# Indices of the first four heads made ahead, and the first gathers moved to the end of the wq stage

## The chip, the cores and the metric

The kernel runs on one core of a Trainium2 chip. The metric is the device time of one execution in microseconds (us); lower is better. The core has five engines, each with an instruction stream of its own that it works through in order: TensorE (PE) multiplies matrices, VectorE (DVE) and ScalarE (ACT) work element by element, GpSimd (POOL) here issues gathers, and SyncE (SP) issues plain loads. Sixteen DMA engines move the data. PEld in a profile is the loading of weights into PE.

## The reference

One layer of a diffusion backbone. Its last part, the one that matters here, is a retrieval network over 256 tokens `ht` with 8 heads and the 16 best experts of 16384 for each head and token:

```python
q = (ht @ wq).reshape(n, PEER_HEADS, 2, PEER_DK // 2)
s = jnp.einsum('nhpc,pkc->nhpk', q, keys)
s1, i1 = lax.top_k(s[:, :, 0], 16)
s2, i2 = lax.top_k(s[:, :, 1], 16)
cand = (s1[..., :, None] + s2[..., None, :]).reshape(n, 8, 256)
sc, ci = lax.top_k(cand, 16)
e = take(i1, ci // 16) * 128 + take(i2, ci % 16)      # 128 experts per token
gate = softmax(sc)
a = jnp.einsum('nd,nhkd->nhk', xb, u_tab[e])          # dots with rows of u
w = gate * gelu(a)
out = jnp.einsum('nhk,nhkd->nd', w, v_tab[e])         # weighted rows of v
```

Tables u and v have 16384 rows of 2048 floats (8 KB a row).

## The kernel before

All arithmetic is in float32; a matrix product is made from a high part (`hi`, an ACT copy to a shorter format) and a low part (`lo`, a DVE subtraction) of each weight block. The stages follow each other: modulation, mixers, output projection `wout`, and then

- **wq**: 16 strips of `wq` (two halves each). After each strip its scores against the keys are made, and DVE takes the best 16 (`score_top`, `pair_top`). When strip 8 is done, `gen_look(1, 0, ...)` turns the best pairs of the first four heads of token block 1 into expert numbers (`e12`).
- **the dense stage**: for 192 of the 256 tokens (`NA`) the dots with all rows of u are made on PE, in 128 rounds that are called rows below. A row needs 1 MB of `u_t`, which comes as two halves; each half takes an ACT instruction that makes `hi` and a DVE instruction that makes `lo` (three `hi` and three `lo` buffers). PE does 16 matmuls with `hi` and 16 with `lo` for a row (tile `ups`); ACT (`ut`) and DVE (`W<-ut,ups`) then store the result in row i2 of the large tile W.
- beside it, the **gathered tokens**: the other 64 tokens, the last of block 1, go in two groups of 32 through 32 steps each. A step u gathers 128 rows of u (1 MB, `DMA_INDIRECT` on POOL) and takes their dot with `hB` on DVE (a SCALAR_TENSOR_TENSOR of 128x2048, called a dot below); a step v gathers 128 rows of v and multiplies them on PE into `adaps` or `yb`. Eight steps u come first, then steps u and v alternate. `gen_route(1, ...)` makes the expert numbers of the last four heads, the list of indices `idx` and the gates, and then starts `gen_gather`.
- **the tail**: for each of the 192 tokens one gather of 128 rows of v and four matmuls (`y`).

What stands where is set when the program is written, by a clock of estimated PE time: generators ("lanes") give up control with a number of microseconds, and their next instructions are put behind the PE work that stands at that time (`spawn`, `pump`, `advance`). Each engine then has a fixed list.

W is filled row by row, so its still empty parts ("rooms" of 2048 columns, 10.67 rows each) hold other things: `wides` is the list of places for a row of u_t, and `gaths` that for gathers. Before the change, rooms 0, 4, 6, 8, 9 (`LENT_1`) and a place of its own (`g1`) hold u_t rows 0 to 5 first, which are loaded beside wq, one per strip (`ahead`), and rooms 1, 2, 3, 5, 7 (`LENT_U`) rows 6 to 10. When its first row is used up, a `LENT_1` place or `g1` becomes a place for gathers.

`gen_gather` spreads its steps evenly up to the estimated end of the dense stage, `R["u_end"]`, which `open_w` sets when the dense stage begins. A gather is issued when its place is free; SP holds the loads in the order of the list.

Of the kernel before, what the change touches and what calls it, by code (L numbers as in the profile page):

```python
# [23 lines left out]
F32 = mybir.dt.float32  # L24
F32R = mybir.dt.float32r
BF16 = mybir.dt.bfloat16
I32 = mybir.dt.int32
U32 = mybir.dt.uint32
AF = mybir.ActivationFunctionType
OP = mybir.AluOpType  # L30
PSUM = bass.MemoryType.PSUM

P = 128
D = 2048
KD = D // P
T = 256
# [4 lines left out]
NK = 128  # L41
PH = 8
TOPK = 16
NB = 64
NA = T - NB
BT = 32
REP = P // BT
STEPS = PH * TOPK // REP
# [15 lines left out]
HY3 = 6.0  # L64
HY4 = 3.0
LOOK_AT = 8
LOOK_Y = 3.0
ITY = 6.0
BIGB = 3
VWY = 7.0  # L70
# [66 lines left out]
class Slots:  # L137
# [11 lines left out]

        self.slots.append([pool, tag, F32, None, True, free, None])  # L150

    def place(self, owner, view, last=None, free=None):

        self.slots.append([owner, view, None, None, True, free, last])

    def over(self, owner):

        return all(s[3] is not None and self.done(s[3]) for s in self.slots if s[0] == owner)

    def take(self, unit):  # L160
        for s in self.slots:
# [21 lines left out]
def build(tc, a, stack, dbg=None):  # L183
# [6 lines left out]
    def open_pool(name, side="left", **kw):  # L190
        cm = tc.tile_pool(name=name, bufs=1, side=side, reuse_waits="tile", **kw)
        return cm, cm.__enter__()
# [120 lines left out]
    def spawn(lane, gen, front=False):  # L313
        q = lanes.setdefault(lane, collections.deque())
        (q.appendleft if front else q.append)([clock["t"], gen])
# [721 lines left out]
    R = {}  # L1037
    gaths = Slots(lambda u: u.used, 2048)


    LENT_1 = (0, 4, 6, 8, 9)
    LENT_U = (1, 2, 3, 5, 7)
    LENT = (4, 6, 8, 9, 10, 11)
    x1d = tc.dram_tile([P, KD, T], F32, name="x1_spill")
# [1 line left out]
    def make_hf(u):  # L1046
        drain(only=("ada",))
        x1 = Y["x"]
        ss = mm_ps("ss1")
        mm(ss[:, 0:T], ones, Y["sq"], start=True, stop=False)  # L1050
        mm(ss[:, 0:T], ones, Y["last"], start=False, stop=True)
        prepare()
        rs = con.tile([P, T], F32, name="rs1", tag="rs1")
        rstd_of(rs, ss[:, 0:T], D)
        araws.drop(V["B"])
        close_pool(V["pb"])
        R["rh"] = open_pool("rh", side="right")
        R["rsb"] = open_pool("rsb", side="right")
        R["rs"] = open_pool("rs", side="right")
        H, S, SB = R["rh"][1], R["rs"][1], R["rsb"][1]  # L1060
        hf = H.tile([P, KD, 2, T], F32R, name="hf", tag="hf")
        hB = H.tile([P, D], F32, name="hB", tag="hB")
        R.update(hB=hB, hf=hf, hfs=hf.rearrange("p k s t -> p s k t"))
        R["keys"] = S.tile([P, 2, NK], F32, name="keys")
        sync.dma_start(R["keys"], a["keys"])
        sync.dma_start(x1d, x1)
        dump("x1", x1)
        n2 = 2 * PH * TOPK
        R["val"] = SB.tile([P, 2, n2], F32, name="val")
        R["ix"] = SB.tile([P, 2, n2], U32, name="ix")  # L1070
        R["sc"] = SB.tile([P, PH, TOPK], F32, name="sc")
        R["ci"] = SB.tile([P, PH, TOPK], U32, name="ci")
        R["e12"] = SB.tile([P, 3, PH, TOPK], F32, name="e12")
        R["h64"] = S.tile([P, KD, NB], F32, name="h64")
        shift, hm = mod[:, 3, 0], {}

        def scaled(k):
            hm[k] = S.tile([P, T], F32, name="hm1", tag="hm1", bufs=4)
            vec.scalar_tensor_tensor(hm[k], x1[:, k], gm[:, 2, k:k + 1], rs, op0=OP.mult, op1=OP.mult)

        skew(KD, scaled,
             lambda k: act.activation(hf[:, k, 0], hm[k], AF.Identity, bias=shift[:, k:k + 1]),
             lambda k: vec.scalar_tensor_tensor(hf[:, k, 1], hm[k], shift[:, k:k + 1],
                                                hf[:, k, 0].bitcast(F32), op0=OP.add, op1=OP.subtract))
        spawn("hA", copy_hB())

        close_pool(pa)
        R["w"] = open_pool("w")
        R["W"] = R["w"][1].tile([P, NK, NA], F32, name="W")
        flat = R["W"].rearrange("p e n -> p (e n)")  # L1090
        room = [flat[:, c * 2048:(c + 1) * 2048] for c in range(NK * NA // 2048)]
        R["room"], R["scr"] = room, room[11]
        R["s0"] = room[10].rearrange("p (h k) -> p h k", k=NK)
        for n, i in enumerate(LENT_1):
            wides.place(("first", i), room[i], n)
        R["g1"] = open_pool("g1")
        wides.slots.append([R["g1"][1], "gath", F32, None, True, None, len(LENT_1)])
        for i in LENT_U:
            wides.place(("row", i), room[i], i * 2048 // NA - 3)
        for i in LENT[:-2]:  # L1100
            gaths.place(("lent", i), room[i], NK, lambda i=i: wides.over(("first", i)))
        gaths.take_over(R["g1"][1], "gath", lambda: wides.over(R["g1"][1]))

    hBd = tc.dram_tile([NB, D], F32, name="hB_spill")

# [104 lines left out]
    def q2_done(hp):  # L1210
        def f(ps):
            S = R["rs"][1]
            at_most(1, "score")
            q = S.tile([P, T], F32, name="q2", tag="q2", bufs=2)
            act.activation(q, ps[:, 0:T], AF.Copy)

            def g():
                yield 2.0
                pk = sm_ps("sc")
                for blk in range(2):  # L1220
                    mm(pk[:, blk * P:(blk + 1) * P], q[:, blk * P:(blk + 1) * P], R["keys"][:, hp % 2],
                       start=True, stop=True)
                s = S.tile([P, NK], F32, name="s", tag="s", bufs=4)
                act.activation(s, pk[:, P:T], AF.Copy)
                act.activation(R["s0"][:, hp], pk[:, 0:P], AF.Copy)
                R[hp] = s
                yield 1.5
                if hp % 2:
                    score_top(1, (hp - 1, R.pop(hp - 1)), (hp, R.pop(hp)))
                yield 0.0  # L1230
                if hp % 4 == 3:
                    pair_top(1, hp // 2 - 1)
                    yield 0.0
                if hp == LOOK_AT:
                    spawn("look", gen_look(1, 0, LOOK_Y))
            spawn("score", g())
        return f

    def gen_top(blk, rp):
# [5 lines left out]
            yield rp  # L1245
        yield from gen_look(blk, 0, rp / 2)

    def gen_route(blk, rp):
        if blk == 1:
            it = con.tile([P, 1152], F32, name="iT", tag="st")  # L1250
            R["iT"] = it[:, 0:3 * T].rearrange("p (s t) -> p s t", s=3)
            R["eA"] = it[:, 3 * T:3 * T + NA].bitcast(I32)
            R["idx"], R["gB"], R["aB"] = (
                it[:, c:c + 2 * STEPS].rearrange("p (b s) -> p b s", b=2)
                for c in range(3 * T + NA, 1152, 2 * STEPS))
            R["idx"] = R["idx"].bitcast(I32)
            ib = con.tile([P, 2 * T], BF16, name="ib", tag="rs1")
            R["i1b"], R["idb"] = ib[:, 0:T].rearrange("p (b c) -> p b c", b=2), ib[:, T:T + P]
            vec.tensor_copy(R["idb"], ident)
        yield from gen_look(blk, 1, rp)  # L1260
        sc, e12 = R["sc"], R["e12"]
        sm, e = R["scr"][:, 0:PH], R["scr"][:, 16:16 + P]
# [3 lines left out]
        act.activation(sc, sc, AF.Exp)  # L1266
        e12f = e12.rearrange("p s h j -> p s (h j)")
        if blk == 1:

            lo = P - NB  # L1270
            vec.scalar_tensor_tensor(e[lo:P], e12f[lo:P, 0], float(NK), e12f[lo:P, 1], op0=OP.mult, op1=OP.add)
            for g in range(2):
                for r in range(REP):
                    vec.tensor_copy(R["idx"][r * BT:(r + 1) * BT, g],
                                    e[lo + g * BT:lo + (g + 1) * BT, r * STEPS:(r + 1) * STEPS])
            spawn("gather", gen_gather())
        vec.tensor_copy(R["i1b"][:, blk], e12f[:, 0])
        yield 1.0
        vec.tensor_reduce(sm, sc, axis=mybir.AxisListType.X, op=OP.add)
# [3 lines left out]
        if blk == 1:  # L1283
            for g in range(2):
                for r in range(REP):
                    vec.tensor_copy(R["gB"][r * BT:(r + 1) * BT, g],
                                    e12f[P - NB + g * BT:P - NB + (g + 1) * BT, 2, r * STEPS:(r + 1) * STEPS])
            R["gates"] = True
        yield max(ITY, vec.t + MARG - clock["t"])
        pt = sm_ps("it")  # L1290
# [99 lines left out]
    to_get = collections.deque()  # L1390

    def fetch():
        while to_get and gather(*to_get[0]):
            to_get.popleft()

    def add_rows(y, w, g, first, last):
# [8 lines left out]
    def gen_gather():  # L1405
# [10 lines left out]
        ops.insert(ops.index(("v", 0, n - SUB)) + 2, ("hB", 1, 0))  # L1416
        for kind, b, s in ops:
            if kind in ("u", "v"):
                to_get.append((a[kind + "_rows"], R["idx"][:, b, s:s + 1]))
        scaled = {}  # L1420

        def scale(b, s):
# [4 lines left out]
        yield FIRST_ROWS  # L1427
        for j, (kind, b, s) in enumerate(ops):
            if kind == "v" and b == 1 and s == n // 2:
                to_get.extend((a["v_rows"], R["eA"][:, t:t + 1], True) for t in range(NA))  # L1430
            if kind == "fin":
                while "gates" not in R:
                    yield 1.0
# [9 lines left out]
            if kind == "hB":  # L1443
                R["hB"] = R["rh"][1].tile([P, D], F32, name="hB", tag="hB")
                load_hB(1)
                continue
            fetch()
            g = got.popleft()
            if kind == "u":
                vec.scalar_tensor_tensor(g.raw, g.raw, 1.0, R["hB"], op0=OP.mult, op1=OP.mult,  # L1450
# [5 lines left out]
                    scale(b, s + 1)  # L1456
            fetch()

            yield max(0.5, (R["u_end"] - clock["t"]) / (len(ops) - j))

    for i2 in range(NK):
        for i in LENT:
# [37 lines left out]
    for g, (k0, nk) in enumerate(GROUPS):  # L1500
# [22 lines left out]
        def place(j):  # L1523
            k, i = k0 + j // 2, j % 2
            return k, i, (xL, xC)[i], (gm[:, i, k:k + 1], mod[:, 0, i, k:k + 1])
# [259 lines left out]
```

## Time and profile before

| what | value |
|---|---|
| median of three runs | 1889.81 us (1889.63 to 1890.5) |
| the profiled execution | 1888.43 us, span 1886.6 us |
| busy in the span | PE 89%, DVE 65%, ACT 37%, POOL 20% |
| mean granted TensorE clock | 0.954 |
| DMA | 672.79 MB, mean 357 GB/s |

The span runs from the first to the last instruction of the profile; the execution's own time has 1.8 us more around it. Busy shares are means over stages with different limits, so the argument reads single stretches: wq runs to about 716 us, the dense stage from there to about 1396 us, and the tail from there to the end.

### The profile page before, as it was taken

To read this page: it belongs to the slowest core of one execution; us is meant where nothing else is said; L and a number is where in the kernel's file an instruction comes from. 1 tells how busy PE (TensorE), PEld (TensorE's weight loads), DVE (VectorE), ACT (ScalarE), POOL (GpSimd) and SP (SyncE) were. 2 spreads that over 40 slices of the span, in tenths; PEclk is the share of its full clock that TensorE was granted. 3 is DMA by queue.
4 is the path that set the end of the run, shared out by engine and by line. 5 is a ranking of instruction groups with operands and counts; after the bars stand their busy time and mean duration, and the time that the engine had idled before them with its cause. 6 is when DMAs were issued, how large, how long until landed. Compare 5 with 4: busy or idle time off the path is not lost.

```text
span 1886.6 us, 29258 instructions
## 1 busy us (share of the span) xinstructions
PE 1678.3 (89%) x11520; PEld 1331.0 (71%) x11520; DVE 1223.2 (65%) x2502; ACT 689.5 (37%) x1093; POOL 379.8 (20%) x334
## 2 busy tenths in 40 slices
PE   5899999999898998999999999999997777777676
PEld 3689779979898998988888789888772222222221
DVE  5256868887898689989997687777553323323232
ACT  4235325656644544544444444444431100101010
POOL 0000000000000001233222233223223333333331
PEclk9999999999999999999999999999998888888987
DMA  9976778988697872999999999999989999999997
GB/s 394 389 284 195 251 269 289 316 301 273 233 378 283 287 274 106 420 396 406 410 409 415 373 407 421 420 421 420 398 344 419 421 420 421 421 421 421 420 421 297
DMA packets 116698, 672.79 MB, mean 357 GB/s; under 512 B 13000, under 2 KB 15816, under 8 KB 53968
## 3 DMA queue, kind: packets, MB, share of 16 engines
q1 hardware_dynamic: 69776, 333.24, 47.2%
q0 software_dynamic: 46784, 337.68, 43.6%
q8 instruction: 90, 1.47, 0.3%
q14 instruction: 48, 0.39, 0.1%
HBM read 666.13 MB, written 4.73 MB: 356 GB/s over the span
## 4 chain that ended last, share of the span: by engine, by line
PE 64%; DMA 23%; DVE 6%; issue 5%; ACT 1%; POOL 1%; SPq 0%; POOLq 0%; ACTq 0%; DVEq 0%
PE ups L358 26%; PE mm L358 25%; DMA gath<-in_v_rows,iT 8%; DMA rawB<-in_v_rows,iT 6%; PE adaps L358 3%; DMA rawA<-in_v_rows,iT 2%; PE y L358 2%; DVE lo L133 2%; DMA ring<-in_ada 2%; DMA raw<-in_v_rows,iT 2%; PE yb L358 1%; PE sm L358 1%; PE num L358 1%; DMA raw<-in_u_t 1%; DMA W<-in_u_t 1%
## 5 line engine op out<-in xcount | busy, mean ns | idle before, releaser
L358 PE MATMUL ups<-hf,hi 128*128 128x384 f32 x2048 | 599.1, 364 | 0.0
L358 PE MATMUL ups<-hf,lo 128*128 128x192 f32 x2048 | 514.5, 251 | 10.0 <-DVE lo L133 10.0
L358 PEld LDWEIGHTS ups<-hf,hi 128*128 128x128 f32 x2048 | 384.5, 188 | 53.1 <-issue 47.0
L358 PEld LDWEIGHTS ups<-hf,lo 128*128 128x128 f32 x2048 | 391.0, 191 | 14.7 <-DVE lo L133 14.0
L133 DVE TENSOR_TENSOR lo<-rawB,hi 128x1024 fp32r<-128x1024 f32 x146 | 178.3, 1222 | 100.0 <-ACT hi L133 87.7
L133 DVE SCALAR_TENSOR_TENSOR oh<-c,iT,pick 128x128 f32<-128x128 f32 x192 | 55.4, 344 | 285.2 <-PE pick L358 285.2
L133 DVE TENSOR_TENSOR lo<-rawA,hi 128x1024 fp32r<-128x1024 f32 x146 | 178.2, 1222 | 90.6 <-ACT hi L133 85.2
L133 ACT ACTIVATE hi<-rawA 128x1024 fp32r<-128x1024 f32 x146 | 154.1, 1056 | 169.1 <-PE mm L358 60.3
L133 ACT ACTIVATE hi<-rawB 128x1024 fp32r<-128x1024 f32 x146 | 154.1, 1056 | 161.3 <-PE ups L358 64.4
L358 PE MATMUL mm<-xL,hi 128*128 128x256 f32 x864 | 180.1, 289 | 6.1 <-ACT xL L133 3.0
L1385 POOL DMA_INDIRECT gath<-in_v_rows,iT x117 | 133.6, 1142 | 246.9 <-PE y L358 116.3
L133 DVE SCALAR_TENSOR_TENSOR adacc<-araw,early,adacc 128x1024 f32<-128x1024 f32 x120 | 152.5, 1278 | 3.2 <-DMA araw<-in_ada 3.2
L358 PEld LDWEIGHTS mm<-xL,hi 128*128 128x128 f32 x864 | 144.9, 193 | 11.0 <-ACT xL L133 3.1
L358 PE MATMUL y<-gath,wA 128*32 128x512 f32 x672 | 102.2, 696 | 48.5 <-DMA gath<-in_v_rows,iT 48.2
L133 ACT ACTIVATE uA<-uA 128x4 f32<-128x4 f32 x48 | 9.9, 205 | 361.5 <-DVE oh L133 361.5
L1385 POOL DMA_INDIRECT W<-in_u_rows,iT x34 | 51.8, 1525 | 412.7 <-ACT hi L133 296.0
L358 PE MATMUL mm<-xL,lo 128*128 128x256 f32 x432 | 122.6, 284 | 0.0
L358 PEld LDWEIGHTS pick<-W,oh 128*128 128x128 f32 x384 | 79.5, 254 | 57.0 <-issue 55.4
L133 ACT ACTIVATE hi<-W 128x1024 fp32r<-128x1024 f32 x78 | 82.6, 1059 | 97.6 <-PE ups L358 86.9
L133 DVE TENSOR_TENSOR lo<-W,hi 128x1024 fp32r<-128x1024 f32 x78 | 94.6, 1219 | 18.4 <-ACT hi L133 17.2
L358 PE MATMUL mm<-hf,hi 128*128 128x256 f32 x512 | 98.4, 291 | 6.1 <-ACT hf L133 5.3
L358 PE MATMUL pick<-W,oh 128*128 128x128 f32 x384 | 97.6, 411 | 1.1 <-issue 1.1
(273 smaller groups left out, 2864.5 us busy)
## 6 DMA issues: line engine op xcount, KB each, us to landing
araw<-in_ada SPq DMA_DIRECT2D x128, 512.0 KB
W<-in_u_t SPq DMA_DIRECT2D x39, 1024.0 KB
rawB<-in_u_t SPq DMA_DIRECT2D x35, 1024.0 KB
rawA<-in_u_t SPq DMA_DIRECT2D x34, 1024.0 KB
ring<-in_ada SPq DMA_DIRECT2D x32, 1024.0 KB
raw<-in_u_t SPq DMA_DIRECT2D x19, 1024.0 KB
rawB<-in_wout SPq DMA_DIRECT2D x16, 512.0 KB
rawA<-in_wout SPq DMA_DIRECT2D x16, 512.0 KB
```

The lines of the kernel that those rows point to most:

```text
L133: return f(*args, **kw)
L358: ten.matmul(out, lhsT, rhs, start=start, stop=stop, skip_group_check=True, **kw)
L1385: pool.indirect_dma_start(out=g.raw, out_offset=None, in_=tab, in_offset=bass.IndirectOffsetOnAxis(ap=idx, axis=0))
```

## The change

The expert numbers of the first four heads are turned into the first 16 steps' indices at once (`place_rows(0)` in `gen_first`), and `gen_gather` starts there, still in the wq stage; `place_rows(1)` in `gen_route` makes the other 16. So that half of the heads is half of the steps, partition and step of an element change places (`r::REP` in place of `r * STEPS:(r + 1) * STEPS`); the gates follow. The steps of `gen_look` for the first half follow each other faster (`LOOK_Y`), and steps of the gathers before `u_end` is known come `DOTS` = 7 us of estimated time apart. Rooms 4, 6, 8, 9 and `g1` hold gathers from the start; room 0 holds row 0 alone, and rows 1 to 5 go to `LENT_U`.

```diff
-LOOK_Y = 3.0
+LOOK_Y = 1.5
+DOTS = 7.0
...
-        for n, i in enumerate(LENT_1):
-            wides.place(("first", i), room[i], n)
-        R["g1"] = open_pool("g1")
-        wides.slots.append([R["g1"][1], "gath", F32, None, True, None, len(LENT_1)])
+        wides.place(("row", 0), room[0], 0)
         for i in LENT_U:
             wides.place(("row", i), room[i], i * 2048 // NA - 3)
+        R["g1"] = open_pool("g1")
+        gaths.add(R["g1"][1], "gath", F32, 1)
         for i in LENT[:-2]:
-            gaths.place(("lent", i), room[i], NK, lambda i=i: wides.over(("first", i)))
-        gaths.take_over(R["g1"][1], "gath", lambda: wides.over(R["g1"][1]))
+            gaths.place(("lent", i), room[i], NK)
...
                 if hp == LOOK_AT:
-                    spawn("look", gen_look(1, 0, LOOK_Y))
+                    spawn("look", gen_first())
...
+    def place_rows(half):
+        n = PH * TOPK // 2
+        lo, c = P - NB, slice(half * n, (half + 1) * n)
+        e12f = R["e12"].rearrange("p s h j -> p s (h j)")
+        e = R["scr"][:, 16:16 + n]
+        vec.scalar_tensor_tensor(e[lo:P], e12f[lo:P, 0, c], float(NK), e12f[lo:P, 1, c], op0=OP.mult, op1=OP.add)
+        for g in range(2):
+            for r in range(REP):
+                vec.tensor_copy(R["idx"][r * BT:(r + 1) * BT, g, half * STEPS // 2:(half + 1) * STEPS // 2],
+                                e[lo + g * BT:lo + (g + 1) * BT, r::REP])
+        R["ready"] = (half + 1) * STEPS // 2
+
+    def gen_first():
...
+        vec.tensor_copy(R["idb"], ident)
+        yield from gen_look(1, 0, LOOK_Y)
+        place_rows(0)
+        spawn("gather", gen_gather())
+        yield 0.0
...
-        while to_get and gather(*to_get[0]):
+        while to_get and to_get[0][0] < R["ready"] and gather(*to_get[0][1:]):
             to_get.popleft()
...
-            yield max(0.5, (R["u_end"] - clock["t"]) / (len(ops) - j))
+            yield max(0.5, (R["u_end"] - clock["t"]) / (len(ops) - j)) if "u_end" in R else DOTS
```

DVE's list, at the beginning of the dense stage. First before the change, from the low part of the second half of row 4 on; `lo..<-W` and `lo..<-gath` are low parts of u_t halves, `W<-ut,ups` stores a row, and the COPY and CASTs are `gen_route`:

```order
L133 TENSOR_TENSOR lo1_7313<-W_5842,hi1_7311 128x1024
L133 TENSOR_REDUCE e12_5772<-W_5842 128x64
L133 TENSOR_TENSOR lo2_7334<-gath_6207,hi2_7332 128x1024
L133 TENSOR_TENSOR W_5842<-ut_7336,ups_7293 128x192
L133 COPY W_5842<-sc_5770 128x8
L133 TENSOR_TENSOR sc_5770<-sc_5770,W_5842 128x128
L133 SCALAR_TENSOR_TENSOR W_5842<-e12_5772 64x128
L133 CAST iT_7152<-W_5842 32x32 x8
```

The same place after the change, from the low part of the first half of row 4 on:

```order
L134 TENSOR_TENSOR lo0_7308<-W_5842,hi0_7306 128x1024
L134 TENSOR_TENSOR W_5842<-ut_7310,ups_7264 128x192
L134 TENSOR_TENSOR W_5842<-W_5842 128x1024
L134 TENSOR_TENSOR lo1_7333<-W_5842,hi1_7331 128x1024
L134 TENSOR_REDUCE e12_5772<-W_5842 128x64
L134 SCALAR_TENSOR_TENSOR W_5842,iT_6649<-W_5842,hB_5764 128x2048
L134 TENSOR_TENSOR lo2_7357<-W_5842,hi2_7355 128x1024
L134 TENSOR_TENSOR W_5842<-ut_7359,ups_7313 128x192
L134 COPY W_5842<-sc_5770 128x8
```

The row with `hB` is a dot, the fourth; in the list of before the first dot stands behind the low parts of row 8. In the list of after a dot stands ahead of the first low part of each of the rows 2 to 9, and the next one ahead of row 13 or 14; before, eight dots stand with the rows 9 to 16.

POOL's list of before, from the first gather on:

```order
L1385 DMA W<-in_u_rows,iT 128x2048 x4
L1385 DMA gath<-in_u_rows,iT 128x2048
L1385 DMA gath_7406<-in_u_rows,iT 128x2048
L1385 DMA W<-in_u_rows,iT 128x2048 x3
L1385 DMA W<-in_v_rows,iT 128x2048
```

The same of after:

```order
L1391 DMA gath_6987<-in_u_rows,iT 128x2048
L1391 DMA W<-in_u_rows,iT 128x2048 x4
L1391 DMA gath_7203<-in_u_rows,iT 128x2048
L1391 DMA gath_7206<-in_u_rows,iT 128x2048
L1391 DMA W<-in_u_rows,iT 128x2048 x2
L1391 DMA W<-in_v_rows,iT 128x2048
```

The order of the gathers stays; the first five now wait for the indices alone, where the first four of before wait also for ACT's `hi` of the u_t rows that lie in their rooms. On SP five loads of u_t fall out of the wq stage and come later.

## Rows read from the trace of the kernel before

**Rows 1.** The page: busy tenths of PE and of DMA in 40 slices.

```profile
PE   5899999999898998999999999999997777777676
DMA  9976778988697872999999999999989999999997
```

**Rows 2.** Stretches: busy us (instructions) per engine, granted clock, DMA share, GB/s.

```profile
core 0: us, PE busy (x) PEld busy (x) DVE busy (x) ACT busy (x) POOL busy (x), PEclk, DMA share, GB/s
...
680.00:716.00 36.00, 35.35 (x298) 34.94 (x298) 33.00 (x107) 15.76 (x29) 0.00 (x0) 1.00 0.66 248
716.00:765.00 49.00, 44.75 (x304) 43.08 (x303) 44.92 (x114) 23.86 (x33) 8.63 (x7) 1.00 0.38 152
765.00:798.00 33.00, 32.28 (x225) 31.89 (x224) 32.46 (x36) 17.50 (x23) 11.77 (x7) 1.00 1.01 419
798.00:1017.00 219.00, 219.00 (x1527) 195.94 (x1526) 202.97 (x429) 102.76 (x153) 66.56 (x46) 1.00 0.99 406
1017.00:1118.00 101.00, 95.31 (x650) 84.07 (x649) 70.12 (x82) 45.30 (x67) 30.52 (x20) 1.00 1.01 392
1118.00:1396.00 278.00, 276.64 (x1926) 244.22 (x1925) 191.99 (x208) 126.96 (x192) 81.95 (x56) 1.00 0.99 406
1396.00:1873.00 477.00, 341.08 (x2144) 135.09 (x2141) 160.47 (x729) 40.73 (x88) 174.53 (x185) 0.86 1.01 418
```

**Rows 3.** The tile ups: matmuls with hi, ns min/median/max, first and last start.

```profile
L358 PE MATMUL ups<-hf,hi x2048: 355/362/448, 716.2 to 1395.5; 128*128 128x384 f32 x187
```

**Rows 4.** ACT in order of time, at the ends of rows 8, 9, 15, 57, 74 and 127.

```profile
764.90 0.31 ACT L133 ACTIVATE ut<-ups 128x192 f32<-128x192 f32 x1
...
769.49 0.31 ACT L133 ACTIVATE ut<-ups 128x192 f32<-128x192 f32 x1
...
798.16 0.31 ACT L133 ACTIVATE ut<-ups 128x192 f32<-128x192 f32 x1
...
1016.83 0.33 ACT L133 ACTIVATE ut<-ups 128x192 f32<-128x192 f32 x1 [1.32 <-PE ups L358]
...
1118.01 0.31 ACT L133 ACTIVATE ut<-ups 128x192 f32<-128x192 f32 x1
...
1395.98 0.33 ACT L133 ACTIVATE ut<-ups 128x192 f32<-128x192 f32 x1 [4.25 <-PE ups L358]
```

**Rows 5.** DVE in order of time, 710 to 763 us: low parts, waits, the first dot.

```profile
710.12 1.22 DVE L133 TENSOR_TENSOR lo<-W,hi 128x1024 fp32r<-128x1024 f32 x1
...
723.56 1.22 DVE L133 TENSOR_TENSOR lo<-W,hi 128x1024 fp32r<-128x1024 f32 x1
...
753.25 1.23 DVE L133 TENSOR_TENSOR lo<-W,hi 128x1024 fp32r<-128x1024 f32 x1 [0.66 <-ACT hi L133]
756.34 1.23 DVE L133 TENSOR_TENSOR lo<-W,hi 128x1024 fp32r<-128x1024 f32 x1 [1.86 <-ACT hi L133]
...
758.15 1.23 DVE L133 TENSOR_TENSOR lo<-W,hi 128x1024 fp32r<-128x1024 f32 x1 [0.31 <-ACT hi L133]
759.29 2.28 DVE L133 SCALAR_TENSOR_TENSOR W<-W,hB 128x2048 f32<-128x2048 f32 x1
...
761.50 1.22 DVE L133 TENSOR_TENSOR lo<-W,hi 128x1024 fp32r<-128x1024 f32 x1
```

**Rows 6.** DVE by groups, 716 to 765 us: busy us, mean ns of one.

```profile
L133 DVE TENSOR_REDUCE e<-W 128x64 f32<-128x1024 f32 x2 | 2.4, 1216 | 0.0
L133 DVE COPY iT<-e 32x32 f32<-32x32 f32 x8 | 1.6, 198 | 0.1
L133 DVE CAST iT<-W 32x32 int32<-32x32 f32 x8 | 1.4, 174 | 0.1
```

**Rows 7.** POOL in order of time: the first gather, and one for a place that a dot freed.

```profile
744.77 1.05 POOL L1385 DMA_INDIRECT W<-in_u_rows,iT  x1 [296.05 <-ACT hi L133]
...
761.85 1.68 POOL L1385 DMA_INDIRECT W<-in_u_rows,iT  x1 [8.60 <-DVE W L133]
```

**Rows 8.** SP's DMA issues in order of time: u_t behind wq, and the reload of hB.

```profile
709.10 0.33 SPq L272 DMA_DIRECT2D rawA<-in_u_t  x1
754.51 14.72 SPq L272 DMA_DIRECT2D W<-in_u_t  x4
...
1033.26 1.83 SPq L1126 DMA_DIRECT2D hB<-hB_spill  x4
1038.63 0.35 SPq L272 DMA_DIRECT2D rawA<-in_u_t  x1
```

More of the change, by code (lines that the diff above doesn't have):

```diff
@@ L150, in take_over, with place @@
         self.slots.append([pool, tag, F32, None, True, free, None])
[L152 to L158, printed above, removed]
+    def place(self, owner, view, last=None):
+        self.slots.append([owner, view, None, None, True, None, last])
     def take(self, unit):
@@ L1038, in build @@
     gaths = Slots(lambda u: u.used, 2048)
-    LENT_1 = (0, 4, 6, 8, 9)
     LENT_U = (1, 2, 3, 5, 7)
@@ L1246, in gen_top @@
         yield from gen_look(blk, 0, rp / 2)
-    def gen_route(blk, rp):
[L1249 to L1259, printed above, removed]
+    def place_rows(half):
[10 more added lines that the diff above has]
+    def gen_first():
+        it = con.tile([P, 1152], F32, name="iT", tag="st")
+        R["iT"] = it[:, 0:3 * T].rearrange("p (s t) -> p s t", s=3)
+        R["eA"] = it[:, 3 * T:3 * T + NA].bitcast(I32)
+        R["idx"], R["gB"], R["aB"] = (
+            it[:, c:c + 2 * STEPS].rearrange("p (b s) -> p b s", b=2)
+            for c in range(3 * T + NA, 1152, 2 * STEPS))
+        R["idx"] = R["idx"].bitcast(I32)
+        ib = con.tile([P, 2 * T], BF16, name="ib", tag="rs1")
+        R["i1b"], R["idb"] = ib[:, 0:T].rearrange("p (b c) -> p b c", b=2), ib[:, T:T + P]
+        vec.tensor_copy(R["idb"], ident)
[3 more added lines that the diff above has]
+        yield 0.0
+    def gen_route(blk, rp):
         yield from gen_look(blk, 1, rp)
@@ L1268, in gen_route @@
         if blk == 1:
[L1270 to L1276, printed above, removed]
+            place_rows(1)
         vec.tensor_copy(R["i1b"][:, blk], e12f[:, 0])
@@ L1286, in gen_route @@
                     vec.tensor_copy(R["gB"][r * BT:(r + 1) * BT, g],
-                                    e12f[P - NB + g * BT:P - NB + (g + 1) * BT, 2, r * STEPS:(r + 1) * STEPS])
+                                    e12f[P - NB + g * BT:P - NB + (g + 1) * BT, 2, r::REP])
             R["gates"] = True
@@ L1418, in gen_gather @@
             if kind in ("u", "v"):
-                to_get.append((a[kind + "_rows"], R["idx"][:, b, s:s + 1]))
+                to_get.append((s, a[kind + "_rows"], R["idx"][:, b, s:s + 1]))
         scaled = {}
@@ L1429, in gen_gather @@
             if kind == "v" and b == 1 and s == n // 2:
-                to_get.extend((a["v_rows"], R["eA"][:, t:t + 1], True) for t in range(NA))
+                to_get.extend((0, a["v_rows"], R["eA"][:, t:t + 1], True) for t in range(NA))
             if kind == "fin":
@@ L1447, in gen_gather @@
             fetch()
+            while not got:
+                yield 1.0
+                fetch()
             g = got.popleft()
```

## The prediction

> **What bounds the kernel now.** I read the page's slices first. PE is at 9 tenths almost throughout until three quarters of the span and at 7 behind that, and DMA, low around the middle of wq, is at 9 behind the dip [rows 1]. Both look like the limit, so the next view is the stretches. In the dense stage PE is busy 219.00 of 219 us (798 to 1017) and 276.64 of 278 (1118 to 1396) at a granted clock of 1.00: PE sets the pace there, although DMA stands at 0.99. Behind 1396 PE is busy 341 of 477 us, DMA moves 418 GB/s: the tail is set by DMA [rows 2]. Its first limits are places, not indices: 185 gathers stand in it [rows 2], so only 7 of the 192 were issued ahead.
>
> The reader is to see next where in the dense stage PE does *not* set the pace. A row's end is its `ut`. Rows 8 to 9 are 4.59 us apart (764.90, 769.49). Rows 16 to 57 take 1016.83 − 798.16 = 218.67; 42 × 4.59 = 192.8, and the list of PE has 24 steps v there, so one costs 25.9 / 24 = 1.08. Nothing is lost. Rows 0 to 8 take 764.90 − 716.2 = 48.7 where 9 × 4.59 = 41.3 would do: **7.4 us are lost**. Rows 9 to 15 take 33.26 instead of 32.1: 1.1 lost. Rows 58 to 74 take 101.18; 17 × 4.59 and 8 steps v are 86.7, so 14.5 are lost. Rows 75 to 127 lose nothing [rows 3, 4].
>
> What is lost in rows 0 to 8 is lost to DVE: it is busy 44.92 of 49 us from 716 to 765, and PE 44.75 [rows 2]. DVE's list is then two low parts and one store a row and, between them, the routing of the last heads. The loss in rows 58 to 74 is another: loads of u_t stand on SP behind `hB`'s reload, the next at 1038.63 [rows 8], and DVE is busy only 70 of 101 us there.
>
> **The change, part by part.**
>
> *Dots moved from rows 9 to 16 into rows 2 to 9.* This is the term that carries the sum. I take one DVE stretch, with the same low parts in both lists: from the low part at 723.56 (row 1, second half) to the one at 761.50 (row 9, first half), 37.94 us. It has 0.66 + 1.86 + 0.31 = 2.83 of waits, all for ACT's `hi`, and one dot, which costs 761.50 − 759.29 = 2.21 from issue to issue [rows 5]. The rest is 37.94 − 2.83 − 2.21 = 32.9. After the change eight dots stand between the same two: 32.9 + 8 × 2.21 = 50.6, if every wait is filled. The low part of row 9 then starts at 723.56 + 50.6 = 774.1 and ends at 775.3; PE ended row 8 at 764.90 before. **Row 9 starts 10.4 us later.** In rows 9 to 15 the dots are gone, so the 1.1 lost there comes back: +9.3. From row 16 on PE is the limit in both, so nothing behind it gives the 9.3 back, except the stall of rows 58 to 74 (a rival). If the waits aren't filled, 2.83 more; if 2 of the dots slip behind row 9 because their gathers are late, 4.4 less. That is 5 to 12.
>
> *Indices of the first half, one strip earlier than row 0.* One reduction of 1.22, a product, eight 32x32 casts of 174 ns [rows 6]: 1.22 + 0.3 + 1.4, about 3 us that stand on DVE ahead of row 0's second low part. The cover is the end of wq on PE: row 0's first low part runs 710.12 to 711.3 [rows 5], its first matmul 716.2 [rows 3], 4.9 us of lead. So nothing; if PE waits for it after all, 3.
>
> *The second eight casts* (each half as wide now). The narrow copies are about as long as wide ones (32x32 COPY 198, CAST 174 [rows 6]); below, half of that. 0.7 to 1.4 us on DVE, in rows 5 to 7. I take the upper end as part of the bound, not of the sum, since the reduction and product that leave these rows (1.5 us) pay for it.
>
> *Faster `LOOK_Y`.* The same instructions, closer together in wq, where DVE is busy 33.00 of 36 us, and PE 35.35 of 36 [rows 2]. Below nothing: 0. Above: 1 us, PE's whole idle time there doubled, 0.65.
>
> *First gathers.* They wait at 744.77 for the last of the `hi` of the lent places; a place freed by a dot is refilled behind the dot (761.85) [rows 7]. After the change they wait for the casts alone, by the sum of the instructions at about 711 to 712 us, 33 us earlier. So "beside wq" is the last 5 us of it. From issue to first dot 759.29 − 744.77 = 14.5 us went by, with four gathers issued at once and DVE in order; a transfer of 1.05 MB at the tail's 418 GB/s is 2.5 us. From 712 the first dot thus finds its data between 714.5 and 726.5. It stands at about 726.5: a wait of 0 to 2 us. I take 0, since the dot of before stood behind other work, too.
>
> *u_t loads that move.* Five rows fall out of the wq stage into the dense stage, where SP's issue of a load into W waited already (754.51, four of them, 14.72 us [rows 8]). Per row 2.5 us of DMA; DMA share is 0.38 from 716 to 765 [rows 2], 30 us free, 5 × 2.5 = 12.5 needed, and the seven gathers 17.5: it just fits. Cost 0; uncovered it would be a row late by one load, 2.5.
>
> *Layout of idx and gates*: the same instructions, 0.
>
> Sum: **+9.3**, of the profiled execution's 1888.43 us (span 1886.6) it makes 1897.7. The median of the runs is 1.4 above that execution, so about **1899** for the median. 0.2% is 3.8 us, about what a measurement of this kernel can tell from no change.
>
> **The rivals.**
>
> *The clock falls.* PE would be busy 41.3 us of the 59 from 716 to 775, 70%; the tail's 341 of 477 is 72%, with 0.86 granted, 716 to 765 was 91%, with 1.00 [rows 2]. If the granted clock goes to 0.86 in rows 2 to 9, their matmuls take up to 41.3 × (1/0.86 − 1) = 6.7 more: 1899 to 1906. Against it: the waits are spread, a few tenths to 2 us each, and PE has slack exactly where it would slow down, so most of it is hidden behind DVE. The Trainium skill ("TensorE: Matmul & The Clock Gate", "HAM oscillation — how this bites in real kernels") describes short idle gaps between groups of matmuls that send the array back to half its clock; the tail's row agrees, the dense stage's rows of before show no case of it.
>
> *The stall of rows 58 to 74 pays it back.* 14.5 us are lost there to late u_t [rows 4], while gathers fill the queue. If the gathers come there with a head start, up to some 6 to 8 of it goes: 1891 to 1893, within 0.2%. Against it: SP's loads wait there in order behind `hB`, whose reload waits for the last dot of the first group, and this moves with the rows.
>
> *Faster: DMA is the limit behind all.* It is at 0.99 to 1.01 from 765 to the end [rows 2]. If that is the true limit, what counts is how many units (1 MB, 2.5 us) are moved ahead of 745 us: before, 13 rows of u_t and no gather; after, about 11 and 7 gathers. Five more, −12.5: 1877. It decides where rows of the dense stage last longer than PE's 4.59 for want of data. Against it: rows 16 to 57 and 75 to 127 lose nothing, so PE spends any lead in data; and the tail starts with what fits in the free places. The Trainium skill ("Perfetto Trace Analysis", "Identifying the Most-Contended Engine") says to optimise first the engine with the highest occupancy, for DMA judged by the utilization of HBM; by it DMA comes first in this stretch and the change would gain. PE's 219.00 of 219 beside it is why I hold it for less likely.
>
> *The change doesn't do what it says.* The first gathers land late, as the 14.5 us from issue to dot allow, and the dots, ahead in DVE's list, make the low parts behind them wait: 2 us at the first, less at the next, about 5 in all: 1904.
>
> **How the numbers follow.** DVE's crowding as summed, 1899, with its own range of 1895 to 1902 from the 5 to 12 above: 0.53. Clock: 0.10. Stall pays back: 0.16. DMA's lead: 0.18. Late gathers: 0.03. Faster by over 0.2%: 0.18; within it: 0.16; slower: 0.66. The range leaves out the DMA case and the far end of the clock's: 1886 to 1905.
>
> **What would show it.** Right: first gather issued at 710 to 713; DVE without idle time over some tenths from row 2 to 9; row 9's first matmul with `hi` at 774 to 776; granted clock 1.00 up to there; rows 10 to 57 at 4.59 plus steps v; about 14 us lost in rows 58 to 74; the dense stage's end at 1405; a tail of 477 us. Wrong: if PE ends row 8 before 770, the dots found room that I didn't see (they stand in DVE's idle time, or fewer of them lie there); if the dense stage ends at 1396 or earlier although row 9 was late, the stall gave it back; if the tail is shorter than 470 us, the gathers' lead outlives the dense stage.

## The result and the profile after

The changed kernel takes 1904.72 us (median of 4; 1898.93 to 1908.75) beside 1890.0: a ratio of 1.0075, interval 1.0049 to 1.0102. On another chip the same file gives 1.0045 (1.0030 to 1.0060). The profiled execution took 1898.93 us, span 1897.2, which is 10.6 more than before. The time moved the way that was forecast and lies in the range of 1886 to 1905, but near its upper end, 5.7 us above the 1899; the profiled execution, the shortest of the four, took 1898.93 where the sum gave 1897.7 for it.

The stretches of the changed kernel, cut where the parts of the dense stage now end (columns as in [rows 2]):

```profile
680.00:716.00 36.00, 35.88 (x306) 35.67 (x305) 34.91 (x122) 16.62 (x30) 3.85 (x3) 1.00 0.47 153
716.00:775.00 59.00, 47.09 (x283) 44.88 (x282) 57.44 (x124) 21.71 (x30) 15.34 (x10) 0.91 0.87 330
807.00:1026.00 219.00, 219.00 (x1526) 195.95 (x1525) 198.42 (x427) 102.62 (x152) 68.01 (x45) 1.00 0.99 402
1026.00:1128.00 102.00, 98.39 (x668) 86.64 (x667) 76.62 (x87) 46.64 (x68) 29.10 (x20) 1.00 1.00 393
1128.00:1405.00 277.00, 277.00 (x1935) 246.28 (x1934) 188.52 (x206) 127.24 (x191) 77.97 (x54) 1.00 0.99 402
1405.00:1885.00 480.00, 340.26 (x2142) 134.84 (x2139) 160.26 (x729) 40.65 (x88) 174.24 (x185) 0.87 1.01 416
...
730.00:735.00 5.00, 3.58 (x16) 3.58 (x17) 5.00 (x8) 0.01 (x1) 1.67 (x1) 0.71 0.73 259
...
745.00:750.00 5.00, 4.56 (x21) 4.56 (x22) 5.00 (x6) 0.85 (x1) 1.20 (x1) 0.66 0.82 297
...
760.00:765.00 5.00, 2.97 (x14) 2.97 (x15) 5.00 (x6) 0.00 (x0) 1.68 (x1) 0.78 0.38 110
```

One stretch is different in kind: from 716 to 775 DVE is busy 57.44 of 59 us and PE only 47.09, at a granted clock of 0.91 instead of 1.00. DMA, which had the time free there, is at 0.87 instead of 0.38. The stretches behind it look much as in [rows 2]. The last three lines are pieces of that stretch, to which PE's waits below belong.

The tile `ups` of the changed kernel, whose first matmul begins the dense stage; behind it ACT in order of time, the `ut` of rows 9, 57, 74 and 127:

```profile
L355 PE MATMUL ups<-hf,hi x2048: 354/362/579, 717.7 to 1404.4; 128*128 128x384 f32 x187
```

```profile
783.26 0.31 ACT L134 ACTIVATE ut<-ups 128x192 f32<-128x192 f32 x1
...
1031.77 0.33 ACT L134 ACTIVATE ut<-ups 128x192 f32<-128x192 f32 x1 [2.05 <-PE ups L355]
...
1129.36 0.31 ACT L134 ACTIVATE ut<-ups 128x192 f32<-128x192 f32 x1
...
1404.91 0.33 ACT L134 ACTIVATE ut<-ups 128x192 f32<-128x192 f32 x1 [4.25 <-PE ups L355]
```

Counted from the first matmul, row 9 ends at 783.26 − 717.7 = 65.6 us, before at 769.49 − 716.2 = 53.3 [rows 3, 4]. By this count all kernels of this study can be laid beside each other, whatever their earlier stages took:

| kernel | row 9 | row 57 | rows 58 to 74 | rows 75 to 127 | row 127 | span less row 127's end | ratio of times |
|---|---|---|---|---|---|---|---|
| before | 53.3 | 300.7 | 101.2 | 278.0 | 679.8 | 490.6 | 1 |
| after | 65.6 | 314.1 | 97.6 | 275.5 | 687.2 | 492.3 | 1.0075 |
| before_again | 53.3 | 300.6 | 102.6 | 279.0 | 682.2 | 491.4 | 0.9997 |
| again | 65.6 | 314.1 | 98.3 | 276.5 | 688.8 | 490.4 | 1.0045 |
| fill | 64.3 | 312.8 | 99.5 | 276.8 | 689.1 | 492.4 | 1.0049 |
| dots_late | 52.9 | 299.9 | 98.8 | 279.7 | 678.4 | 490.5 | 0.9979 |
| gathers_late | 52.9 | 300.2 | 102.2 | 276.6 | 678.9 | 492.1 | 0.9980 |
| two_early | 57.3 | 304.8 | 101.2 | 277.1 | 683.2 | 492.1 | 1.0025 |
| dots_mid | 55.3 | 303.5 | 99.6 | 277.1 | 680.2 | 490.7 | 1.0001 |
| spread | 49.8 | 297.3 | 103.5 | 281.7 | 682.6 | 491.4 | 1.0006 |
| spread_quarters | 49.8 | 298.4 | 104.5 | 277.5 | 680.4 | 491.4 | 1.0017 |

The profiled columns are of one execution each. Two profiles of the same file agree to 0.1 us at rows 9 and 57; behind row 57 they differ by one or two us in each column, and by up to 2.4 at row 127. The ratios are to the kernel before on the same chip, which varies by chip and run (1890 to 1893 in the medians): the first two rows are from one chip; again, fill, dots_late and gathers_late from a second; before_again, two_early, dots_mid and spread from a third; spread_quarters from a fourth.

Why row 9 is late shows in DVE's list of the changed kernel, from row 1's second low part to row 9's first; of the eight dots three are shown:

```profile
724.97 1.22 DVE L134 TENSOR_TENSOR lo<-W,hi 128x1024 fp32r<-128x1024 f32 x1
...
727.93 2.28 DVE L134 SCALAR_TENSOR_TENSOR gath<-gath,hB 128x2048 f32<-128x2048 f32 x1
730.14 0.08 DVE L134 DVE_READ_ACCUMULATOR gath<-gath,hB 128x1 f32 x1
730.14 1.22 DVE L134 TENSOR_TENSOR lo<-W,hi 128x1024 fp32r<-128x1024 f32 x1
...
753.36 1.44 DVE L134 CAST iT<-W 32x16 int32<-32x16 f32 x8
...
758.54 2.29 DVE L134 SCALAR_TENSOR_TENSOR W<-W,hB 128x2048 f32<-128x2048 f32 x1
760.76 0.08 DVE L134 DVE_READ_ACCUMULATOR W<-W,hB 128x1 f32 x1
760.76 1.22 DVE L134 TENSOR_TENSOR lo<-rawB,hi 128x1024 fp32r<-128x1024 f32 x1
...
772.79 2.28 DVE L134 SCALAR_TENSOR_TENSOR W<-W,hB 128x2048 f32<-128x2048 f32 x1
775.00 0.08 DVE L134 DVE_READ_ACCUMULATOR W<-W,hB 128x1 f32 x1
775.00 1.22 DVE L134 TENSOR_TENSOR lo<-W,hi 128x1024 fp32r<-128x1024 f32 x1
```

From 724.97 to 775.00 are 50.03 us, and no row in between has an idle time in brackets: DVE works without a pause. Before, the same stretch took 37.94 us [rows 5].

PE's list of the changed kernel shows who waits, and what the waits do to the clock:

```profile
728.62 0.36 PE L355 MATMUL ups<-hf,hi 128*128 128x384 f32 x1
731.42 0.36 PE L355 MATMUL ups<-hf,lo 128*128 128x192 f32 x1 [2.43 <-DVE lo L134]
...
732.81 0.58 PE L355 MATMUL ups<-hf,hi 128*128 128x384 f32 x1
...
745.44 0.36 PE L355 MATMUL ups<-hf,lo 128*128 128x192 f32 x1 [1.92 <-DVE lo L134]
...
756.23 0.36 PE L355 MATMUL ups<-hf,lo 128*128 128x192 f32 x1 [1.21 <-DVE lo L134]
...
762.03 0.36 PE L355 MATMUL ups<-hf,lo 128*128 128x192 f32 x1 [3.24 <-DVE lo L134]
```

A matmul with `hi` takes 0.36 us ahead of the first wait shown and 0.58 some 1.4 us behind its end: the lower of the two levels, 1.2 instead of 2.4 GHz. The granted clock by the pieces of 5 us above: 0.71 behind the first of these waits, 0.66 behind the second, 0.78 behind the last.

Behind 762.03 PE doesn't wait for DVE again up to row 15: a row with a dot and without routing costs DVE 4.75 us (760.76, 765.51, 770.26, 775.00 are the starts of first low parts), about PE's 4.59. The routing and the dots together are what is too much, in rows 2 to 6.

### The profile page after: what moved, and what is told of

It is laid out like the page before. It is cut to its first block, busy times and chain, and to the rows that moved or that the text cites. A ratio compares the mean times of both kernels' runs of the same rounds, so it can differ in the third digit from the quotient of the medians.

```text
span 1897.2 us, 29273 instructions
## 1 busy us (share of the span) xinstructions
PE 1682.7 (89%) x11520; PEld 1335.7 (70%) x11520; DVE 1224.6 (65%) x2511; ACT 689.0 (36%) x1093; POOL 379.4 (20%) x334
## 4 chain that ended last, share of the span: by engine, by line
PE 66%; DMA 23%; DVE 6%; issue 4%; ACT 1%; POOL 0%; SPq 0%; POOLq 0%; ACTq 0%; DVEq 0%
PE ups L355 28%; PE mm L355 25%; DMA gath<-in_v_rows,iT 6%; DMA rawA<-in_v_rows,iT 4%; DMA rawB<-in_v_rows,iT 4%; DMA raw<-in_v_rows,iT 4%; PE adaps L355 3%; PE y L355 2%; DMA hB<-in_v_rows,iT 2%; PE yb L355 2%; DMA ring<-in_ada 2%; DVE lo L134 2%; PE sm L355 1%; DVE W L134 1%; PE num L355 1%
## 5 line engine op out<-in xcount | busy, mean ns | idle before, releaser
L355 PEld LDWEIGHTS ups<-hf,lo 128*128 128x128 f32 x2048 | 393.8, 192 | 19.8 <-DVE lo L134 19.3
L134 DVE SCALAR_TENSOR_TENSOR oh<-c,iT,pick 128x128 f32<-128x128 f32 x192 | 55.3, 344 | 287.0 <-PE pick L355 287.0
L1391 POOL DMA_INDIRECT gath<-in_u_rows,iT x29 | 41.3, 1423 | 367.3 <-DVE iT L134 262.4
```

Source lines behind the costliest of these rows:

```text
L134: return f(*args, **kw)
L355: ten.matmul(out, lhsT, rhs, start=start, stop=stop, skip_group_check=True, **kw)
L1391: pool.indirect_dma_start(out=g.raw, out_offset=None, in_=tab, in_offset=bass.IndirectOffsetOnAxis(ap=idx, axis=0))
```

## The experiments

The theory: dots in rows 2 to 6 crowd DVE, and PE waits. Rivals: the clock; the new places of u_t and the gathers; DMA as the limit behind all.

**again**: the changed kernel, nothing edited. 

> The changed kernel once more, nothing edited. Its four times ran from 1898.9 to 1908.8 us where the kernel before keeps within 1 us, and the slower ones had a mean granted clock of 0.950 to 0.951 instead of 0.955. Theory (the waits for DVE in rows 2 to 9 let the granted clock fall, for a time that differs between runs): times between 1898 and 1909 again, and if this profile is one of the slow ones, its granted clock from 716 to 785 us lies under the 0.91 of the first profile. Rival (the spread comes from the tail or from earlier stages): the clock there is 0.91 again, and the difference stands elsewhere.

1902.11 us (1898.7 to 1902.9), ratio 1.0045. Its profile (span 1896.9) repeats rows 0 to 57 to a tenth, and the stretch 716 to 775 has a granted clock of 0.91 again. So the time of rows 0 to 9 is a fixed one; but the profiled execution was the shortest of the six, so none of the longer ones was seen. On this chip the kernel before varied as much, 1890.1 to 1898.6 in 23 runs. The spread is thus not the change's alone; where it arises stays open.

**dots_late**: early indices, early gathers, dots where they were.

```diff
         fetch()
+        while "placed" not in R:
+            yield 1.0
         yield FIRST_ROWS
...
             place_rows(1)
+            R["placed"] = True
```

> The changed kernel with early indices and early gathers, but its first eight dots held back to rows 9 to 16, where the kernel before has them. Theory (DVE in rows 2 to 9 is crowded by the dots): row 9 ends within 2 us of where the kernel before ends it, counted from the start of the dense stage, and the time is 1888 to 1892 us with a spread under 2 us. Rival 1 (the new places of the u_t rows or the early gathers cost the time): 1898 or more, as the changed kernel. Rival 2 (DMA is the limit behind all, and the dots hid its gain): the seven gathers moved ahead show now, 1877 to 1884.

1889.51 us, ratio 0.9979 (0.9969 to 0.9989); row 9 at 52.9. The spread, 5.3 us, is larger than expected. This one edit takes back all that the change cost. The stretch 716 to 776 of this kernel:

```profile
716.00:776.00 60.00, 55.65 (x382) 53.79 (x381) 55.91 (x136) 28.48 (x42) 9.95 (x8) 1.00 0.78 294
```

PE is busy 55.65 of 60 at 1.00, while DMA still has its early work (0.78). The 12.5 us that the DMA rival promised are not there: 0.2% is 4 us, and with its interval 6 at most. But the run tests that rival only in part, since the lead in bytes doesn't last. The kernel before and this one, from 60 us ahead of the first matmul of `ups` to 28.6 us behind it, and for 24.4 us from there:

```profile
656.20:744.80 88.60, 86.18 (x678) 84.05 (x676) 76.23 (x251) 40.73 (x69) 0.03 (x1) 1.00 0.51 184
744.80:769.20 24.40, 21.92 (x152) 21.66 (x153) 21.33 (x33) 11.85 (x17) 10.29 (x8) 1.00 0.94 376
```

```profile
659.40:748.00 88.60, 86.21 (x679) 84.10 (x677) 77.74 (x261) 41.24 (x69) 7.44 (x6) 1.00 0.67 230
748.00:772.40 24.40, 22.31 (x155) 22.06 (x156) 21.64 (x33) 12.11 (x18) 3.35 (x2) 1.00 0.68 241
```

By GB/s times us this is 20.4 MB for 16.3 at the first point and 26.3 for 25.5 at the second: of a lead of 4.1 MB, 0.8 is left at row 9, while DMA is at 0.68. The first six gathers fill the places, and POOL's seventh waits 40.98 us for a dot (763.11). So a head start of the gathers alone is worth next to nothing here; what a lead in bytes would be worth if it were kept is not shown.

**gathers_late** was to start the gathers late as well.

```diff
         place_rows(0)
-        spawn("gather", gen_gather())
         yield 0.0
...
             place_rows(1)
+            spawn("gather", gen_gather())
```

> The changed kernel with indices of the first half made early and the new places of u_t, but the gathers and dots started where the kernel before starts them. It moves less than both kernels ahead of row 4: five rows of u_t less than before, seven gathers less than after. If dots crowding DVE is the cause, row 9 ends where it did before, and the time is 1889 to 1892. If the amount that DMA has moved by then counts (12.5 us behind the kernel before), 1900 to 1903.

It didn't do that. POOL has nothing ahead of them in its list, so its first gather went out at 711.76 all the same, when the indices stood:

```profile
711.76 1.94 POOL L1391 DMA_INDIRECT gath<-in_u_rows,iT  x1 [262.49 <-DVE iT L134]
```

It is dots_late a second time: 1889.61 us, ratio 0.9980 (0.9968 to 0.9992), row 9 at 52.9. What less early DMA would cost wasn't tried.

**fill**: dummy matmuls in PE's waits, to keep the clock.

```diff
+FILL = {(2, 0): 11, (4, 0): 8, (5, 1): 4, (6, 0): 14}
...
+                if kt == 0 and (i2, half) in FILL:
...
+                    for _ in range(FILL[i2, half]):
+                        ten.matmul(R["fill"][:, 0:2 * NA]..., hi[:, kt], h, start=True, stop=True)
```

> The changed kernel with 37 more matmuls of 128x384 into an unused PSUM tile (their results are not used), put where PE waits for low parts: 11 in row 2, 8 in row 4, 4 in row 5, 14 in row 6. DVE's list is the same. If the half clock in these rows costs what the first profile shows (matmuls at half speed from 762.8 to 766.0 us, some 1.5 us behind the last wait), the granted clock of the stage is 1.00, the best time is 1897 to 1898 and the spread shrinks to 1 or 2 us. If the spread of the changed kernel comes from elsewhere, the times still run over 10 us. If PE itself is the limit in these rows, the time grows by 5 to 7 us.

```profile
716.00:776.00 60.00, 52.70 (x335) 50.24 (x335) 58.42 (x126) 22.79 (x31) 15.92 (x12) 0.97 0.86 331
```

The granted clock of the stretch rose to 0.97, not 1.00, and row 9 ended at 64.3, 1.3 us earlier. The whole time did not fall (1902.63) and its spread of 4.7 us did not vanish. So what the clock costs of row 9's delay is 1.3 us as far as this run takes it back (the last 0.03 of the clock were not tried). The rest of the time at the lower level would then lie in front of the next wait for DVE, where it costs nothing.

**two_early**: two dots ahead of rows 2 and 3, six late.

```diff
+            R["placed"] = True
...
+            if j == 2:
+                while "placed" not in R:
+                    yield 1.0
+                yield FIRST_ROWS
```

> The changed kernel with two of the eight first dots left early (ahead of rows 2 and 3), six held back to rows 9 to 14. DVE's sum: 2 x 2.21 more in the stretch to row 9, less the 2.8 us of waits that they can fill, is 1.6; row 9 ends 54 to 56 us behind the first matmul (52.9 with all eight late, 65.6 with all early), time 1890 to 1893. If it is the early start as such that costs (gathers and dots in the same rows), not their number: nearer to 65.

1896.42 us, ratio 1.0025 (1.0016 to 1.0035), row 9 at 57.3, both outside what was expected: two dots cost 4.4 us at row 9, 2 x 2.21, where I had set 1.6. My mistake was to let them fill the waits that DVE has in rows 7 to 9. Those are for ACT's `hi`, which waits for PE; when PE is held back ahead of them they move along with it, and 2.29 us of them are left in this trace. The eight dots of the changed kernel, which stand in these rows too, leave none.

**dots_mid**: all eight dots right behind the routing, ahead of rows 7 to 13.

```diff
-        yield FIRST_ROWS
+        yield 4.0
```

(on dots_late) 

> The changed kernel with all eight first dots right behind the routing: ahead of rows 7, 8, 9, 9, 10 to 13, two rows or less earlier than in the kernel before. DVE's sum: three more dots up to row 9 than with late dots, 6.6 less 2.8 us: row 9 ends at 54 to 57 us, of which a part comes back by row 15, since two dots fewer stand behind; time 1890 to 1892. If early dots cost the same wherever they stand, row 9 is at 60 or more.

1891.7 us, ratio 1.0001 (0.9992 to 1.0010), row 9 at 55.3. Three more dots up to row 9 cost 2.4 there, 0.8 each; in this trace they fill the waits of rows 7 to 9, of which none is left. So a dot behind the routing costs less than half of one beside it: the place counts, as the theory has it.

**before_again**: the kernel before on another chip. 

> The kernel before, nothing edited, for a profile of it on the chip of the experiments, where its times ran from 1890.1 to 1898.6 us. All theories: rows 0 to 9 of the dense stage take 53.3 us again, counted from its first matmul. If the new places of u_t rows are worth something of their own (the two versions with late dots had medians of 1889.5 and 1889.6 there, the kernel before 1893.3), the difference stands in rows 57 to 127, above all in row 63, which took 12.7 us in the first profile and 5 to 8.6 in all others.

Rows 0 to 57 repeat to a tenth (53.3, 300.6), row 63 took 10.7. Rows 58 to 127 took 381.6 us, in the first profile 379.2, and with late dots 378.5 and 378.7. The two profiles of before alone differ by 2.4, so the new places show no worth of their own. PE's first matmul behind the pause of about 5 us, at the beginning of wq and ahead of all that the change touches, starts at 607.87 here, in the first profile of before at 606.06 and in the changed kernel at 607.74:

```profile
607.87 1.18 PE L358 MATMUL mm<-hf,hi 128*128 128x256 f32 x2 [5.28 <-ACT hf L133]
```

So the 1.5 us that the changed kernel's dense stage starts later (717.7 for 716.2) are not the change's.

**spread**: the remedy that the theory suggests. Since the first 16 steps have their indices, the other heads' routing is not urgent.

```diff
-RP1 = 2.0
+RP1 = 5.0
...
-DOTS = 7.0
+DOTS = 9.2
...
-RT_DELAY = 60.0
+RT_DELAY = 30.0
...
+            if "u_end" not in R or j < SUB:
+                yield DOTS
...
```

> The changed kernel with the load on DVE made even instead: the routing of the last four heads, whose indices the first 16 steps no longer need, is spread over rows 1 to 12 (RP1 5 instead of 2, RT_DELAY 30 instead of 60), and the first eight dots come 9.2 us apart, ahead of rows 2, 5, 7, 9 and so on to 17. If DVE's crowding is what costs in rows 0 to 9, of the kernel before too (7.4 us lost there), row 9 ends at 48 to 50 us and the time is 1884 to 1887, below both kernels. If PE is held back by something else there, 52 to 53 and 1889 to 1891. If the later end of the routing delays something, more than 1892.

```profile
716.00:776.00 60.00, 56.99 (x393) 55.77 (x392) 56.48 (x108) 28.55 (x38) 12.07 (x9) 1.00 0.91 354
```

Row 9 ended at 49.8, as the theory said, and at row 57 the lead over dots_late was 2.6 us. The time was 1894.11 us, ratio 1.0006 (0.9997 to 1.0015): rows 58 to 127 took 385.2 instead of 378.5. By its number the last branch came (more than 1892, the routing's later end delays something); no run tells it from a stage behind that takes any lead back. A lead in rows 0 to 57 is not kept, as a part of the delay there was not either.

**spread_quarters**: spread, with `hB`'s reload in four parts.

```diff
-        ops.insert(ops.index(("v", 0, n - SUB)) + 2, ("hB", 1, 0))
+        at = ops.index(("v", 0, n - SUB)) + 2
+        for r in range(REP):
+            ops.insert(at + 2 * r, ("hB", 1, r))
...
-                load_hB(1)
+                load_hB(1, (s,))
```

> The version with the routing spread, with the reload of hB for the second group of gathered tokens issued in four quarters (256 KB each, one to three of them between loads of u_t) instead of 1 MB at one place. Theory: the load of u_t that stands behind the reload on SP comes late and costs a row 12.6 us there (row 64 with the routing spread, row 63 in the kernel before), so rows 57 to 74 take 97 to 100 us instead of 103.5, the 3 us gained in rows 0 to 9 stay, and the time is 1885 to 1889, 3 to 6 below the kernel before. Rival (DMA, or the pace of 4.97 us a row behind row 64, takes any lead back): rows 57 to 74 take 102 to 104 again, and the time is 1891 to 1895.

1892.89 us, ratio 1.0017 (1.0008 to 1.0025); rows 58 to 74 took 104.5, row 64 11.2. The rival held: the reload at one place is not what takes the lead back. The trace shows what the stalled row waits for:

```profile
1046.06 0.35 SPq L269 DMA_DIRECT2D W<-in_u_t  x1
...
1065.89 1.06 ACT L134 ACTIVATE hi<-W 128x1024 fp32r<-128x1024 f32 x1 [8.44 <-DMA W<-in_u_t]
```

```profile
1025.00:1033.00 8.00, 8.00 (x58) 6.00 (x57) 5.21 (x7) 4.14 (x7) 0.94 (x1) 1.00 1.02 420
1048.00:1058.00 10.00, 10.00 (x72) 8.00 (x71) 5.85 (x7) 4.38 (x8) 2.72 (x2) 1.00 1.02 317
```

This load of u_t is read 19.8 us after its issue, and ACT waits for it. DMA, at the same share of 1.02, moves 317 GB/s beside the reload instead of 420 ahead of it.

**after_nov, late_nov, spread_nov**: no gathers of v in the dense stage; the steps v multiply `hf` instead, so the results are not the layer's.

```diff
-            if kind in ("u", "v"):
+            if kind == "u":
                 to_get.append(...)
...
+            if kind == "v":
+                g.raw = R["hf"].rearrange("p k s t -> p (k s t)")[:, 0:D].bitcast(F32)
```

> The changed kernel without the 64 gathers of v in the dense stage: its steps v multiply a tile that is in place anyway, so PE, DVE and ACT do the same, and some 67 MB, 160 us at 418 GB/s, are not moved. If DMA limits rows 57 to 127 beside PE and so paid back half of what was lost earlier: rows 57 to 127 take the same time in all three kernels of this call, 10 to 25 us less than the 373 to 375 of the changed kernel, and the changed kernel without gathers of v ends the dense stage 12 us behind the one with late dots. If the stall at the reload of hB alone pays back: rows 57 to 127 take 370 to 375 again.

> The version with late dots, without the 64 gathers of v in the same way. DMA as a second limit: rows 57 to 127 take as long as in the changed kernel without them (379 before); row 9 at 53. Otherwise 378 again.

> The version with the routing spread, without the 64 gathers of v. DMA as a second limit: the 3 us that it gained in rows 0 to 9 stay to the end of the dense stage, 3 us ahead of late dots, and rows 57 to 127 take as long as in the other two (385 before). Otherwise the 3 us are lost there again.

With 64 gathers fewer the three took 1908.1, 1907.6 and 1894.4 us, one run each: no shorter, two of them longer, and the question over rows 57 to 127 is not answered as put (379.7, 389.6 and 384.5 us). Their rows 63 alone took 13.9, 20.0 and 16.7. In late_nov DVE stood there with a dot that waited for the reload, and the low parts behind it waited too:

```profile
1057.06 2.29 DVE L134 SCALAR_TENSOR_TENSOR W<-W,hB 128x2048 f32<-128x2048 f32 x1 [8.74 <-DMA hB<-hB_spill]
```

Rows 75 to 127, free of that, do tell something. They took 276.8, 277.7 and 278.7 us, with the gathers 275.5 to 281.7. Most of this stretch without gathers (late_nov), and with them (dots_late):

```profile
1130.00:1405.00 275.00, 275.00 (x1916) 242.97 (x1915) 192.20 (x209) 129.51 (x193) 35.08 (x22) 1.00 0.76 283
```

```profile
1126.00:1397.00 271.00, 270.04 (x1881) 238.97 (x1880) 185.37 (x201) 124.09 (x184) 83.72 (x54) 1.00 0.98 400
```

A DMA share of 0.76 instead of 0.98 and the same pace: there DMA is busy, but it is not the limit.

## Why the prediction was right, and where not

*Dots into rows 2 to 9.* Right in place, kind and nearly in size. DVE's stretch was to take 50.6 us and took 50.03; row 9 was to be 10.4 us later and was 12.2 (65.55 and 53.32 us). Of the rest 1.3 is the clock (fill), which I had kept apart as a rival with 0.86 and up to 6.7 us; it came as a part of the same event, at 0.91. The sign "granted clock 1.00 up to there" was thus wrong, while DVE without idle time and the first gather came as told. In one more detail the step was wrong: I looked at the last low part, of row 9, but the last wait that holds PE is that of row 6, at 762.03.

*1.1 us back in rows 9 to 15.* Right, but hidden. From row 9's end to row 15's both kernels took 28.7 us. In the changed one a step v stands in this stretch (row 14, 802.9 us; the first of before is in row 18, 808.6), and a row with a step v takes some 1.1 us more: without it the 1.1 had come back. By row 57 the changed kernel has two steps v more behind it than the kernel before, so of its delay of 13.4 us there about 2.2 are steps that only stand earlier, and 11.2 are lost. (For the price of a step v I had counted 24 in rows 16 to 57; by PE's own matmuls it is 23. No term of the sum hangs on it.)

*Rows 58 to 127.* I had written that "nothing behind it gives the 9.3 back, except the stall of rows 58 to 74 (a rival)": the exception came true in part. Rows 58 to 74 took 97.6 instead of 101.2, and rows 75 to 127 275.5 instead of 278.0, together 6.0 us less. About 2.2 of them are the two steps v; so some 3.8 of 11.2 us were paid back, and 7.4 were left at the dense stage's end.

That the sum of 9.3 came so near to the 10.6 of the profile is in part luck. The delay was larger than summed (11.2 for 9.3), a rival that the sum leaves out took 3.8 off it, and 1.5 us ahead of the dense stage and 1.7 in the tail came on top, both no more than two profiles of one file differ by. The medians of the other runs of the file lie 4 and 6 us above its two profiled ones, and no trace shows where; so of the 14.7 us between the medians only the profile's 10.6 is accounted for.

*Indices, casts, gathers.* Right: first gather at 711.48 (forecast 711 to 712), first dot at 727.93 without a wait (726.5), the second eight casts 1.44 us, PE busy 35.88 of the 36 us to 716. No cost, and 33 us of head start that buy at most the 0.2% of dots_late.

*DMA behind all* fell where PE sets the pace: in rows 16 to 57 (PE busy 219.00 of 219 us at a DMA share of 0.99, before and after) and in rows 75 to 127 (late_nov). In the rows between, the traces point at DMA. A row's `ut` stands on ACT behind a `hi` that may wait, so take PE's last matmul of a row instead: in the seven kernels before, before_again, dots_late, gathers_late, dots_mid, spread and spread_quarters, row 57 ends 297.0 to 303.2 us behind the first matmul, and row 74 ends 396.6 to 398.1 in all seven. Whatever lead PE has at row 57 is thus gone at row 74. `hi` waits for loads of u_t there, as in the first fence of spread_quarters. Rows 64 to 71, less 1.1 us for each step v, take 39.3 to 46.4 us in all kernels with gathers of v, and 37.0 in each of the three without, which is 8 times 4.59 and 0.3. But those three come to these rows behind a longer stall, in which loads can collect, and spread_nov ends row 74 at 398.0 all the same. So that the transfers take the lead back fits most of this and isn't shown by an experiment of its own; what is excluded is the size of the reload's single load (spread_quarters).

## What to carry to other kernels

Work that is made ready earlier should not therefore be issued earlier on an engine with a fixed list: a dot cost 0.8 us behind the routing (dots_mid) and 2.2 us beside it (two_early). Before an instruction is moved up, count what its engine has to do in that row beside what the pacing engine needs (here 4.59 us); only what fits is free. And a gain of 3 us in one part of a stage is worth nothing until one knows that the next part doesn't wait for something else.

## What was not expected of the hardware

A wait of about 2 to 3 us on PE was followed by matmuls of 0.57 to 0.58 us instead of 0.36, three times within 40 us, in a stretch whose granted clock is 0.91. Yet with DVE as the limit this cost some 1.3 us of 12. And a DMA share of 1.02 says little of the rate: beside the reload of `hB` it went with 317 GB/s, ahead of it with 420.
